# Four matmuls of a partition sum issued together, and a substitution issued in three runs, in the second mixer of a two-block transformer kernel

## The chip, the cores and the metric

The kernel runs on one core of a Trainium2 chip. The metric is device microseconds for one execution, which takes in two transformer blocks. TensorE (PE) does the matmuls, VectorE (DVE) and ScalarE (ACT) the elementwise work, GpSimd (POOL) hardly any; SyncE (SP) issues most DMAs. Each engine works through its own queue in order, and waits there for what its next instruction needs.

## The reference

Everything is float32, with 512 tokens and a model width of 1024. Two blocks follow each other; each is a feed-forward, a mixer and a feed-forward, with residuals and norms. The second block's mixer is the part that is changed. Its input projection has 28 slices of 128 columns (12 of a short convolution, 12 of q, k and v, 4 of z) and 8 columns for beta and the decay.

```python
def gated_delta_rule_chunked(q, k, v, g, beta):
    ...
    g = jnp.cumsum(g.reshape(bsz, n, c, nh).transpose(0, 3, 1, 2), axis=-1)
    decay = jnp.exp(jnp.where(causal, gdiff, -jnp.inf))
    lower = jnp.where(strict, jnp.einsum('bhncd,bhnsd->bhncs', k_beta, k) * decay, 0.0)
    rhs = jnp.concatenate([v_beta, k_beta * jnp.exp(g)[..., None]], axis=-1)
    sol = lax.linalg.triangular_solve(lower, rhs, left_side=True, lower=True, unit_diagonal=True)
    u, w = sol[..., :dv], sol[..., dv:]
    attn_intra = jnp.where(causal, jnp.einsum('bhncd,bhnsd->bhncs', q, k) * decay, 0.0)
    ...
    def step(state, inp):
        q_c, k_c, u_c, w_c, a_c, gl = inp
        v_new = u_c - jnp.einsum('bhck,bhkv->bhcv', w_c, state)
        o_c = jnp.einsum('bhck,bhkv->bhcv', q_c, state) + jnp.einsum('bhcs,bhsv->bhcv', a_c, v_new)
        state = state * gl[..., None, None] + jnp.einsum('bhck,bhcv->bhkv', k_c, v_new)
        return state, o_c
```

q, k and v go through a causal convolution of 4 taps and a silu; q and k are scaled to unit length per head (a sum of squares over the head's 128 channels, which lie on the partitions here); the head's output goes through an RMS norm (again such a sum) and a gate silu(z). The short convolution has 3 taps and a norm in 8 groups of 64 channels. There are 4 heads of 128 channels.

## The kernel before

A product of float32 matrices is made of three matmuls of split values (hi x wh, lo x wh, hi x wl), so that a projection of 1024 inputs by 128 outputs over 512 tokens is a pass of 24 matmuls (`gproj`, L819), each with 512 columns. A pass is read out by VectorE with the norm's scale (L1001, L1011, L1014, L1026). The weights of a pass arrive by DMA and are split by ScalarE (wh, L198) and VectorE (wl, L199).

In the second mixer (`mix2`) PE's order is written by hand. `main()` runs through the 28 passes and yields after each matmul; after each one `tick()` (L1042) steps at most one generator whose lag has run out. Such generators are the chain of a head (`chain`), of which up to three run at once, the end of a short convolution (`short_end`) and the decays. A generator issues work for all engines up to its next `yield`, and the number that it yields, out of the table `LAG`, is how many ticks (projection matmuls) go by before it is stepped again. The Tile scheduler puts the instructions of VectorE and ScalarE into an order of its own, fixed when the kernel is built.

A head's chain takes these steps, named by the lag behind them:

- entry: the decay (`decay`: spread of columns L267, gl L791, er L793, dec L796 and L799), transposes of k (L836), kd and ke (L838, L839), squares of k and q (c0);
- the key-query product L848, masked scores `at` (L850), q scaled by er (L851) (c1);
- the sum of squares of k, four matmuls of one column each (L714 in `tok_sums`), a reciprocal square root by Newton steps on VectorE (L240 to L253) (c2);
- the key-key product L864, u (L867) (c3), transposes of v L872, vi (L873) (c5);
- the preparation of the substitution of 16 x 16 blocks (L881 to L892), transposes of u L899 (c6);
- the substitution: products by block L905 and L906, evicted by ScalarE into bx (L907), then 15 turns of two small VectorE operations (L913, L915), then zu (L917) (c7);
- three merge levels (L925, L927, L932, L933, L937; zu renewed at L938) (c8, c9), the product with ke, L942, evicted as wt (L944) (c10);
- a scan over four groups of tokens: pv (L953, L955), vn (L956), po (L958, L967), pst (L962), st (L966) (r0, r1); the sum of squares of the output (o0), its spread and the gate (o1).

PSUM tiles with tag "g" share three banks (`bank`), which every step above asks for in turn; a step waits until the bank's last tile has been read. The silu and the exponential lie in different activation tables; an ACT_TABLE_LOAD stands ahead of an activation whose table is not the one loaded.

Of the kernel before, what the change touches and what calls it, by code (L numbers as in the profile page):

```python
# [30 lines left out]
LIVE = 3  # L31
NWARM = 9
SCRATCH = 1024
LAG = dict(d0=4, d1=30, d2=81, d3=7, d4=10, tok=1, c0=7, c1=3, c2=3, c3=2, c5=17, c6=26, c7=46, c8=11, c9=9, c10=11, r0=3, r1=4, o0=9, o1=27, s0=14, s1=22)
MIXORD = (4, 5, 6, 0, 1, 2, 3, 7)
WINDOWS = (2, 4, 8, 16)
MAGIC = float(0x5F3759DF)
# [87 lines left out]
class Kern:  # L125
# [4 lines left out]
    def nm(self, s):  # L130
        self.n += 1
        return f"{s}_{self.n}"
# [8 lines left out]
def tile_blocks(ctx: ExitStack, tc: tile.TileContext, ins, out, stop=None):  # L141
# [15 lines left out]
    ones1 = const.tile([P, 1], F32, name="ones1")  # L157
    gcomb = const.tile([P, 8], F32, name="gcomb")

    def vcol(name, i=0, n=1):  # L160
        o = VEC_COLS[name][0] + i
        return vec[:, o : o + n]
# [19 lines left out]
    def tmp():  # L182
        return tp.tile([P, T], F32, name=nm("t"), tag="t", bufs=5)

    def stmp():
        return tp.tile([P, T], F32, name=nm("s"), tag="s", bufs=3)
# [50 lines left out]
    def rsqrt_cols(src, n, scale, eps=EPS):  # L237

        v = rp.tile([P, n], F32, name=nm("rv"), tag="rv", bufs=4)
        nc.vector.tensor_scalar(v, src, scale, eps, ALU.mult, ALU.add)  # L240
        return newton(v, n)
# [411 lines left out]
    def mix2(prep, nxt):  # L653
# [3 lines left out]
        with ExitStack() as c:  # L657
            yp = K.pool(c, nm("yc"))
            yc, os_ = [None] * 4, [None] * GH
            with ExitStack() as c2:  # L660
# [12 lines left out]
                def gk(name, i=0):  # L673
                    o, n = CONST_COLS[name]
                    o += i * P - NKEEP
                    return gcst[:, o : o + min(n, P)]
# [3 lines left out]
                groups = gk("groups")  # L680
# [5 lines left out]
                def ct(n):  # L686
                    return cp.tile([P, n], F32, name=nm("c"), tag=f"c{n}", bufs={4: 12, 16: 10}[n])
# [5 lines left out]
                def bank(shape=S):  # L693
                    return psp.tile(shape, F32, name=nm("pg"), tag="g", bufs=3)
# [4 lines left out]
                def th(x):  # L699
                    return x.rearrange("p (t q) -> p t q", q=4)  # L700

                def hb(x):
                    return x.rearrange("p (o q) -> p o q", o=1).to_broadcast([P, NT, 4])
# [4 lines left out]
                def tok_sums(s, n, rhs):  # L708

                    ps = bank([P, NT, n])  # L710
                    for t in range(NT):
                        if t:
                            yield LAG["tok"]
                        nc.tensor.matmul(ps[:, t, :], s[:, t * P : (t + 1) * P], rhs, start=True, stop=True)  # L714
                    return ps

                def spread2(cols, groups=1):
                    ps = bank([P, T])
                    spread_into(ps, cols, groups)
                    return ps  # L720
# [18 lines left out]
                def decays():  # L739

                    yield LAG["d0"]
                    bas = tmp()
                    nc.vector.tensor_tensor(bas[:16], pba[:16], rb[:16], ALU.mult)
                    yield LAG["d1"]
                    pbt = bank([P, NT, 16])
# [26 lines left out]
                    nc.vector.scalar_tensor_tensor(th(g), th(z), -1.0, hb(ea), ALU.mult, ALU.mult)  # L772
                    yield LAG["d2"]

                    pg = bank([P, 16])
                    nc.tensor.matmul(pg, csum, g, start=True, stop=True)
                    nc.vector.tensor_copy(gc, pg)
                    yield LAG["d3"]
                    pg2 = bank([P, 16])
# [4 lines left out]
                    nc.scalar.activation(eg, gc, AF.Exp)  # L784
                    yield LAG["d4"]
                    decayed.append(True)
# [43 lines left out]
                def chain(hd, q, k, v):  # L830
# [9 lines left out]
                    sk = stmp()  # L840
# [11 lines left out]
                    yield LAG["c1"]  # L852

                    irk, es = ct(4), ct(4)
                    pn = yield from tok_sums(sk, 1, ones1)
                    rk = rsqrt_cols(pn.rearrange("p t o -> p (t o)"), NT, 1.0)
                    nc.vector.reciprocal(irk, rk)
                    nc.vector.tensor_tensor(es, rk, rk, ALU.mult)
# [49 lines left out]
                    zc = ep.tile([P, NT, SB], F32, name=nm("zc"), tag="zc", bufs=2)  # L908
                    nc.gpsimd.tensor_copy(zc, gk("d16").rearrange("p (o c) -> p o c", o=1).to_broadcast([P, NT, SB]))
                    for i in range(SB - 1):  # L910
                        sb = ep.tile([P, NT, SB], F32, name=nm("sb"), tag="sb", bufs=2)
                        n = SB - 1 - i
                        nc.vector.tensor_tensor(sb[:, :, :n], bx[:, :, i, i + 1 :],  # L913
                                                zc[:, :, i : i + 1].to_broadcast([P, NT, n]), ALU.mult)
                        nc.vector.tensor_tensor(zc[:, :, i + 1 :], zc[:, :, i + 1 :], sb[:, :, :n], ALU.add)  # L915
# [54 lines left out]
                    so = stmp()  # L970
                    nc.scalar.activation(so, po, AF.Square)
                    nc.vector.tensor_tensor(so, so, o, ALU.add)
                    nc.scalar.activation(o, po, AF.Copy)
                    yield LAG["o0"]
                    pn = yield from tok_sums(so, 1, ones1)
                    ro = rsqrt_cols(pn.rearrange("p t o -> p (t o)"), NT, 1.0 / P, EPS * EPS * P)
                    yield LAG["o1"]
                    pb = spread2(col1(ro))
# [4 lines left out]
                def short_end(i, yy):  # L983
                    sq = stmp()
                    nc.scalar.activation(sq, yy, AF.Square)
                    yield LAG["s0"]
                    pn = yield from tok_sums(sq, 2, groups)
                    cols = rsqrt_cols(pn.rearrange("p t o -> p (t o)"), 2 * NT, 1.0 / 64)
                    yield LAG["s1"]
                    pb = spread2(cols.rearrange("p (t o) -> p t o", o=2), 2)  # L990
                    nc.vector.scalar_tensor_tensor(yy, yy, vcol("conv_out_norm_2", i), pb, ALU.mult, ALU.mult)
                    yc[i] = yy
# [3 lines left out]
                def qkv_of(hd):  # L996
                    qkv = [None] * 3
                    for s in (1, 0, 2):
                        ps = yield from gproj(12 + 4 * s + hd)
                        x_ = tmp()  # L1000
                        nc.vector.tensor_tensor(x_, ps, rb, ALU.mult)  # L1001
                        y = conv(x_, "gdn_conv_w_2", 4 * s + hd, 4)
                        o = (gp if s == 0 else ep).tile([P, T], F32, name=nm("qkv"), tag="q" if s == 0 else "kv", bufs=4 if s == 0 else 3)
                        nc.scalar.activation(o, y, AF.Silu)
                        qkv[s] = o
                    waiting.append(Steps(chain(hd, *qkv)))

                def short_of(i):
                    pa = yield from gproj(4 + i)
                    ca = tmp()  # L1010
                    nc.vector.tensor_tensor(ca, pa, rb, ALU.mult)  # L1011
                    pb_ = yield from gproj(8 + i)
                    chh = tmp()
                    nc.vector.tensor_tensor(chh, pb_, rb, ALU.mult)  # L1014
                    nc.vector.tensor_tensor(chh, chh, ca, ALU.mult)
                    y = conv(chh, "conv_short_w_2", i, 3)
                    pc_ = yield from gproj(i)
                    nc.vector.tensor_tensor(y, y, rb, ALU.mult)
                    yy = yp.tile([P, T], F32, name=nm("yy"), tag="yy", bufs=4)
                    nc.vector.tensor_tensor(yy, pc_, y, ALU.mult)  # L1020
                    shorts.append(Steps(short_end(i, yy)))
# [66 lines left out]
    for what in ("x0", "w00", "x1", "x2", "x3", "w01", "x4", "x5", "x6", "w10", "w11", "x7"):  # L1088
# [4 lines left out]
        else:  # L1093
            i, j = int(what[1]), int(what[2])
# [115 lines left out]
```

## Time and profile before

| | |
|---|---|
| median of 3 runs | 2249.04 us (2247.82 to 2250.24) |
| profiled execution | 2249.06 us |
| its span | 2247.1 us |
| mean granted clock | 0.995 |
| PE busy | 2224.2 us, 99% |
| DVE busy | 1123.8 us, 50% |
| ACT busy | 814.5 us, 36% |

The span is the time between the first and the last instruction; 1.96 us of the execution lie outside it. The second mixer runs in it from 1569.9 us (first L819) to 1829.86 us (first L214 of the output projection). Busy is the time in which an engine worked on an instruction; a matmul's busy time overlaps that of the next, so that the distance of starts says what a matmul costs. The granted clock is that of TensorE, where 1.00 is full speed.

### The profile page before, as it was taken

The numbers are of one execution on the slowest core, as the hardware profiler recorded it, in microseconds if no ns is written. First come the engines' busy times: TensorE is split into PE (matmuls) and PEld (weight loads), VectorE is DVE, ScalarE is ACT, GpSimd is POOL, SyncE is SP. The second block draws the span as 40 slices with busy tenths as digits, with TensorE's granted clock in tenths as the row PEclk, the third lists the DMA queues.
The fourth block names the chain that finished last, engine by engine and source line by source line (L and its number), as shares of the span: only waits on it lengthen the run. The fifth ranks groups of instructions, "written<-read, shape, count | busy, mean of one in ns | idle before, by whom it ended". The sixth has DMA issues, their size and how long they took to land. (4 is left out here: it accounts for less than half of the span.)

```text
span 2247.1 us, 25204 instructions
## 1 busy us (share of the span) xinstructions
PE 2224.2 (99%) x10246; PEld 1847.2 (82%) x10246; DVE 1123.8 (50%) x1701; ACT 814.5 (36%) x1067; POOL 35.9 (2%) x54
## 2 busy tenths in 40 slices
PE   9999999999999999999999999999989999999998
PEld 7888888888888888888888888888778888888887
DVE  6444334565654455444434544433787665444332
ACT  6233223444432234332324332222565344233321
POOL 0000000000220000000000000000000000000000
PEclk9999999999999999999999999999999999999999
DMA  5333333322233232333332333333211123232332
GB/s 165 96 101 94 96 94 112 96 81 85 75 104 102 95 94 96 102 94 99 94 93 90 106 100 94 95 98 102 75 57 38 57 75 94 95 103 94 96 96 71
DMA packets 61476, 208.17 MB, mean 93 GB/s; under 512 B 6832, under 2 KB 9392, under 8 KB 61360
## 3 DMA queue, kind: packets, MB, share of 16 engines
q1 hardware_dynamic: 58832, 203.48, 29.2%
q10 hardware_dynamic: 2528, 3.08, 0.4%
q8 instruction: 80, 1.31, 0.2%
q14 instruction: 36, 0.29, 0.0%
HBM read 204.44 MB, written 2.10 MB: 92 GB/s over the span
## 5 line engine op out<-in xcount | busy, mean ns | idle before, releaser
L214 PE MATMUL ps<-hi,wh 128*128 128x512 f32 (+1 forms) x2774 | 1076.2, 388 | 1.4 <-ACT wh L198 1.3
L215 PE MATMUL ps<-lo,wh 128*128 128x512 f32 (+1 forms) x2774 | 1075.7, 388 | 0.3 <-DVE lo L202 0.3
L216 PE MATMUL ps<-hi,wl 128*128 128x512 f32 (+1 forms) x2774 | 1075.6, 388 | 0.0
L198 ACT ACTIVATE wh<-wr 128x1024 fp32r<-128x1024 f32 (+2 forms) x392 | 407.4, 1039 | 1135.3 <-PE ps L215 613.5
L199 DVE TENSOR_TENSOR wl<-wr,wh 128x1024 fp32r<-128x1024 f32 (+2 forms) x392 | 469.1, 1197 | 332.9 <-ACT wh L198 332.0
L214 PEld LDWEIGHTS ps<-hi,wh 128*128 128x128 f32 x2774 | 521.2, 188 | 109.5 <-ACT wh L198 2.4
L215 PEld LDWEIGHTS ps<-lo,wh 128*128 128x128 f32 x2774 | 521.1, 188 | 108.1 <-DVE lo L202 1.7
L216 PEld LDWEIGHTS ps<-hi,wl 128*128 128x128 f32 x2774 | 521.3, 188 | 107.4 <-DVE wl L199 1.2
L362 DVE TENSOR_TENSOR t<-ps,rb 128x512 f32<-128x512 f32 x88 | 60.8, 691 | 257.4 <-PE ps L216 257.4
L359 DVE TENSOR_TENSOR t<-ps,rb 128x512 f32<-128x512 f32 x88 | 60.8, 691 | 169.5 <-PE ps L216 169.4
L198 ACT ACTIVATE hi<-t 128x512 fp32r<-128x512 f32 x119 | 75.2, 632 | 114.6 <-DVE t L364 63.3
L819 PE MATMUL ps<-hi,wh 128*128 128x512 f32 x224 | 93.6, 418 | 0.3 <-DVE t L1001 0.3
L819 PE MATMUL ps<-hi,wl 128*128 128x512 f32 x224 | 93.0, 415 | 0.0
L819 PE MATMUL ps<-lo,wh 128*128 128x512 f32 x224 | 92.6, 413 | 0.0
L199 DVE TENSOR_TENSOR lo<-t,hi 128x512 fp32r<-128x512 f32 x119 | 83.5, 702 | 6.0 <-ACT hi L198 5.6
L364 DVE TENSOR_TENSOR t<-t,t 128x512 f32<-128x512 f32 x88 | 60.9, 692 | 8.3
L360 ACT ACTIVATE t<-t 128x512 f32<-128x512 f32 x88 | 54.1, 615 | 4.1 <-DVE t L359 4.1
L373 DVE SCALAR_TENSOR_TENSOR h<-ps,h 128x512 f32<-128x512 f32 x31 | 21.4, 692 | 60.4 <-PE ps L216 60.4
L819 PEld LDWEIGHTS ps<-hi,wh 128*128 128x128 f32 x224 | 43.2, 193 | 7.2 <-DVE t L1001 0.8
L819 PEld LDWEIGHTS ps<-hi,wl 128*128 128x128 f32 x224 | 43.2, 193 | 6.7 <-issue 0.2
L819 PEld LDWEIGHTS ps<-lo,wh 128*128 128x128 f32 x224 | 43.1, 192 | 6.6 <-issue 0.2
L808 DVE SCALAR_TENSOR_TENSOR t<-t,vec,t 128x511 f32<-128x511 f32 (+2 forms) x44 | 32.5, 744 | 0.2
(291 smaller groups left out, 1222.2 us busy)
## 6 DMA issues: line engine op xcount, KB each, us to landing
wr<-in_ffn_w_in SPq DMA_DIRECT2D x174, 512.0 KB, 3.5
wr<-in_ffn_w_out SPq DMA_DIRECT2D x64, 512.0 KB, 3.5
wr<-in_w_in SPq DMA_DIRECT2D x48, 512.0 KB, 3.5
wr<-in_w_mix_in SPq DMA_DIRECT2D x28, 512.0 KB, 3.5
wr<-in_ffn_w_out SPq DMA_DIRECT2D x32, 384.0 KB, 3.1
wr<-in_w_v SPq DMA_DIRECT2D x8, 512.0 KB, 3.6
wr<-in_w_ret_up SPq DMA_DIRECT2D x8, 512.0 KB, 3.5
wr<-in_w_pool_up SPq DMA_DIRECT2D x8, 512.0 KB, 3.5
```

Source lines behind the costliest of these rows:

```text
L198: nc.scalar.activation(hi, src, AF.Copy)
L199: nc.vector.tensor_tensor(lo, src, hi.bitcast(F32), ALU.subtract)
L214: nc.tensor.matmul(ps, lh, rh, start=start, stop=False)
L215: nc.tensor.matmul(ps, lh, rl, start=False, stop=False)
L216: nc.tensor.matmul(ps, ll, rh, start=False, stop=stop)
L359: nc.vector.tensor_tensor(g, pg, rb, ALU.mult)
L360: nc.scalar.activation(g, g, AF.Silu)
L362: nc.vector.tensor_tensor(u, pu, rb, ALU.mult)
L364: nc.vector.tensor_tensor(m, g, u, ALU.mult)
L373: nc.vector.scalar_tensor_tensor(h[d], ps, 0.5, h[d], ALU.mult, ALU.add)
L808: nc.vector.scalar_tensor_tensor(y[:, s:], x_[:, : T - s], vcol(names, (kw - 1 - s) * nt + i), y[:, s:], ALU.mult, ALU.add)
L819: nc.tensor.matmul(ps, a[:, k, :], b, start=(k == j == 0), stop=(k == KD - 1 and j == 2))
```

## The change

`tok_sums` issues its four matmuls in one step, with no yield between them, and is a plain function; its three callers (12 calls, 48 matmuls) take its result directly. The loop of 15 turns of the substitution yields before its turns 4 and 9 with the lag c7, which becomes 16 in place of 46; with the yield behind zu it now waits three times. Six other lags grow by 1 or 2, and `tok` goes.

```diff
--- before.py
+++ after.py
@@ -31,7 +31,7 @@
 LIVE = 3
 NWARM = 9
 SCRATCH = 1024
-LAG = dict(d0=4, d1=30, d2=81, d3=7, d4=10, tok=1, c0=7, c1=3, c2=3, c3=2, c5=17, c6=26, c7=46, c8=11, c9=9, c10=11, r0=3, r1=4, o0=9, o1=27, s0=14, s1=22)
+LAG = dict(d0=4, d1=30, d2=81, d3=7, d4=10, c0=9, c1=3, c2=3, c3=2, c5=19, c6=28, c7=16, c8=12, c9=9, c10=11, r0=3, r1=4, o0=10, o1=27, s0=14, s1=22)
 MIXORD = (4, 5, 6, 0, 1, 2, 3, 7)
 WINDOWS = (2, 4, 8, 16)
 MAGIC = float(0x5F3759DF)
@@ -709,8 +709,6 @@
 
                     ps = bank([P, NT, n])
                     for t in range(NT):
-                        if t:
-                            yield LAG["tok"]
                         nc.tensor.matmul(ps[:, t, :], s[:, t * P : (t + 1) * P], rhs, start=True, stop=True)
                     return ps
 
@@ -852,7 +850,7 @@
                     yield LAG["c1"]
 
                     irk, es = ct(4), ct(4)
-                    pn = yield from tok_sums(sk, 1, ones1)
+                    pn = tok_sums(sk, 1, ones1)
                     rk = rsqrt_cols(pn.rearrange("p t o -> p (t o)"), NT, 1.0)
                     nc.vector.reciprocal(irk, rk)
                     nc.vector.tensor_tensor(es, rk, rk, ALU.mult)
@@ -908,6 +906,8 @@
                     zc = ep.tile([P, NT, SB], F32, name=nm("zc"), tag="zc", bufs=2)
                     nc.gpsimd.tensor_copy(zc, gk("d16").rearrange("p (o c) -> p o c", o=1).to_broadcast([P, NT, SB]))
                     for i in range(SB - 1):
+                        if i in (4, 9):
+                            yield LAG["c7"]
                         sb = ep.tile([P, NT, SB], F32, name=nm("sb"), tag="sb", bufs=2)
                         n = SB - 1 - i
                         nc.vector.tensor_tensor(sb[:, :, :n], bx[:, :, i, i + 1 :],
@@ -972,7 +972,7 @@
                     nc.vector.tensor_tensor(so, so, o, ALU.add)
                     nc.scalar.activation(o, po, AF.Copy)
                     yield LAG["o0"]
-                    pn = yield from tok_sums(so, 1, ones1)
+                    pn = tok_sums(so, 1, ones1)
                     ro = rsqrt_cols(pn.rearrange("p t o -> p (t o)"), NT, 1.0 / P, EPS * EPS * P)
                     yield LAG["o1"]
                     pb = spread2(col1(ro))
@@ -984,7 +984,7 @@
                     sq = stmp()
                     nc.scalar.activation(sq, yy, AF.Square)
                     yield LAG["s0"]
-                    pn = yield from tok_sums(sq, 2, groups)
+                    pn = tok_sums(sq, 2, groups)
                     cols = rsqrt_cols(pn.rearrange("p t o -> p (t o)"), 2 * NT, 1.0 / 64)
                     yield LAG["s1"]
                     pb = spread2(cols.rearrange("p (t o) -> p t o", o=2), 2)
```

Lines behind the removed ones have numbers lower by 2: L819 becomes L817, L848 L846, L899 L897, L905 to L907 L903 to L905, L714 L712, L791 L789, L793 L791, L796 L794, L799 L797, L806 L804, L808 L806. The substitution's L913 to L917 and what follows keep theirs.

The change moves work on every engine. The first place is head 1's entry on ScalarE. Before, bx (L907) is evicted ahead of the entry's activations; `c`, `er`, `dec` are head 1's decay, `qkv_11431` its q and `qkv_11529` its v:

```order
L907 ACTIVATE bx_11464<-pg_11465 128x512
L907 ACTIVATE bx_11464<-pg_11469 128x512
L806 ACTIVATE t_11524<-t_11522,vec 128x512
L791 ACT_TABLE_LOAD
L791 ACTIVATE c_11544<-pg_11539 128x4
L1004 ACT_TABLE_LOAD
L1004 ACTIVATE qkv_11431<-t_11426 128x512
L1004 ACTIVATE qkv_11529<-t_11524 128x512
L793 ACT_TABLE_LOAD
L793 ACTIVATE er_11546<-pg_11539 128x512
L843 ACTIVATE o_11566<-qkv_11431 128x512
L799 ACTIVATE dec_11548<-dec_11548 128x512
```

After, where a table load and `c` of L789 stand directly ahead of the first of these rows (`qkv_11431` is q, `qkv_11471` is v):

```order
L1004 ACT_TABLE_LOAD
L1004 ACTIVATE qkv_11431<-t_11426 128x512
L804 ACTIVATE t_11466<-t_11464,vec 128x512
L791 ACT_TABLE_LOAD
L791 ACTIVATE er_11488<-pg_11481 128x512
L841 ACTIVATE o_11508<-qkv_11431 128x512
L1004 ACT_TABLE_LOAD
L1004 ACTIVATE qkv_11471<-t_11466 128x512
L797 ACT_TABLE_LOAD
L797 ACTIVATE dec_11490<-dec_11490 128x512
L905 ACTIVATE bx_11512<-pg_11513 128x512
L905 ACTIVATE bx_11512<-pg_11517 128x512
```

The two evictions of bx have moved from ahead of the entry's activations to behind them, and v's silu is no longer beside q's.

The second place is the end of head 0's substitution on VectorE. `zu_11520` and `zu_11660` are head 0's zu, `ps` is the result of a projection pass, `u_11623` is head 1's. Before:

```order
L915 TENSOR_TENSOR zc_11473<-zc_11473,sb_11517 128x4
L873 TENSOR_TENSOR vi_11561<-pg_11630,c_11586 128x512
L917 TENSOR_TENSOR zu_11520<-zc_11473,gcst_10892 128x512
L859 TENSOR_TENSOR c_11587<-c_11587,c_10915 128x4
L867 SCALAR_TENSOR_TENSOR u_11623<-pg_11618,c_11587,dec_11548 128x128 x4
L883 COPY c_2051_11663<-u_11623 32x128 x2
L886 TENSOR_SCALAR c_2052_11668<-c_2051_11663,gcst_10892 128x64
L887 SCALAR_TENSOR_TENSOR c_2052_11668<-c_2051_11663,gcst_10892,c_2052_11668 128x64
L199 TENSOR_TENSOR lo_11672<-c_2052_11668,hi_11671 128x64
L892 TENSOR_TENSOR xx_11675<-hi_11671,gcst_10892 128x1024
L892 TENSOR_TENSOR xx_11677<-lo_11672,gcst_10892 128x1024
L1001 TENSOR_TENSOR t_11714<-ps_11650,rb_10905 128x512
```

After:

```order
L1001 TENSOR_TENSOR t_11698<-ps_11630,rb_10905 128x512
L913 TENSOR_TENSOR sb_11651<-bx_11512,zc_11521 128x4x3
L199 TENSOR_TENSOR wl_11883<-wr_11880,wh_11882 128x1024
L915 TENSOR_TENSOR zc_11521<-zc_11521,sb_11651 128x4x3
L806 SCALAR_TENSOR_TENSOR t_11700<-t_11698,vec,t_11700 128x511
L913 TENSOR_TENSOR sb_11654<-bx_11512,zc_11521 128x4x2
L806 SCALAR_TENSOR_TENSOR t_11700<-t_11698,vec,t_11700 128x510
L915 TENSOR_TENSOR zc_11521<-zc_11521,sb_11654 128x4x2
L806 SCALAR_TENSOR_TENSOR t_11700<-t_11698,vec,t_11700 128x509
L913 TENSOR_TENSOR sb_11657<-bx_11512,zc_11521 128x4
L915 TENSOR_TENSOR zc_11521<-zc_11521,sb_11657 128x4
L917 TENSOR_TENSOR zu_11660<-zc_11521,gcst_10892 128x512
```

Before, zu stands ahead of u and of the scaling of a pass (L1001); after, it stands behind the scaling, the weight split and the convolution of a pass, with the last three turns of the substitution among them.

The third place is PE at head 0's first merge level (L925), which reads that zu. Before:

```order
L819 MATMUL ps_11650<-hi_10773,wh_11646 128x512
L819 MATMUL ps_11650<-lo_10774,wh_11646 128x512
L819 MATMUL ps_11650<-hi_10773,wl_11647 128x512
L819 MATMUL ps_11650<-hi_10866,wh_11646 128x512
L925 MATMUL pg_11696<-zu_11520,lt_11415 128x128 x4
L927 MATMUL pg_11697<-cst,zu_11520 128x128 x4
L819 MATMUL ps_11650<-lo_10867,wh_11646 128x512
L819 MATMUL ps_11650<-hi_10866,wl_11647 128x512
```

After:

```order
L817 MATMUL ps_11630<-hi_10866,wh_11626 128x512
L817 MATMUL ps_11630<-lo_10867,wh_11626 128x512
L817 MATMUL ps_11630<-hi_10866,wl_11627 128x512
L817 MATMUL ps_11713<-hi_10217,wh_11709 128x512
L817 MATMUL ps_11713<-lo_10218,wh_11709 128x512
L817 MATMUL ps_11713<-hi_10217,wl_11710 128x512
L925 MATMUL pg_11717<-zu_11660,lt_11416 128x128 x4
L927 MATMUL pg_11718<-cst,zu_11660 128x128 x4
```

Before, the merge stands within the pass `ps_11650`, two matmuls ahead of its end; after, it stands three matmuls into the pass that follows `ps_11630`, the pass whose scaling is ahead of zu on VectorE.

## Rows read from the trace of the kernel before

**Rows 1.** The page's first part: busy time, share of the span and instructions of each engine.

```profile
PE 2224.2 (99%) x10246; PEld 1847.2 (82%) x10246; DVE 1123.8 (50%) x1701; ACT 814.5 (36%) x1067; POOL 35.9 (2%) x54
```

**Rows 2.** The second mixer in windows. Columns: the stretch in us, its length, busy us (and instructions) of PE, of PE's weight loads, of VectorE, of ScalarE and of GpSimd, granted TensorE clock, share of the DMA engines, GB/s.

```profile
1630.00:1660.00 30.00, 26.06 (x124) 21.46 (x123) 25.63 (x81) 15.98 (x26) 0.24 (x1) 0.89 0.15 54
1660.00:1690.00 30.00, 27.85 (x172) 24.15 (x171) 23.93 (x68) 18.62 (x31) 0.24 (x1) 1.00 0.17 54
...
1720.00:1750.00 30.00, 26.37 (x164) 23.43 (x163) 22.65 (x75) 15.02 (x28) 0.00 (x0) 0.94 0.11 36
```

**Rows 3.** The table of waits of the second mixer, 1569 to 1850 us, PE's rows alone. Columns: the engine and the line that waited, what it waited for, us in total, times, longest.

```profile
PE pv L955 <- DVE st L966: 3.6, 1, 3.6
...
PE pg L848 <- ACT qkv L1004: 2.2, 1, 2.2
...
PE pg L899 <- DVE u L867: 1.7, 1, 1.7
...
PE pg L927 <- ACT wt L944: 1.1, 1, 1.1
...
PE pg L942 <- DVE dec L796: 0.9, 1, 0.9
```

**Rows 4.** PE's timeline from the transposes of head 1's u to head 0's first merge level. Columns: start in us, us, engine, line, operation, out<-in, tile sizes, count [idle before <-releaser].

```profile
1652.34 1.10 PE L899 MATMUL pg<-cst,u 128*128 128x128 f32 x4 [1.70 <-DVE u L867]
...
1654.09 0.63 PE L819 MATMUL ps<-hi,wl 128*128 128x512 f32 x1
1654.52 0.63 PE L819 MATMUL ps<-hi,wh 128*128 128x512 f32 x1
...
1656.61 0.39 PE L819 MATMUL ps<-hi,wl 128*128 128x512 f32 x1
...
1657.08 0.49 PE L925 MATMUL pg<-zu,lt 128*128 128x128 f32 x3
```

**Rows 5.** PE's timeline, the same columns, at head 1's key-query product.

```profile
1639.23 1.87 PE L848 MATMUL pg<-qkv,qkv 128*128 128x128 f32 x8 [2.25 <-ACT qkv L1004]
...
1644.34 0.40 PE L819 MATMUL ps<-hi,wh 128*128 128x512 f32 x1
```

**Rows 6.** PE's timeline at the key-query product of head 2.

```profile
1679.53 1.06 PE L848 MATMUL pg<-qkv,qkv 128*128 128x128 f32 x8
1680.35 0.47 PE L819 MATMUL ps<-hi,wh 128*128 128x512 f32 x1
```

**Rows 7.** PE's timeline at a sum over partitions of head 0, and at the sums of the last norm (L423), where several stand in a run.

```profile
1616.68 0.48 PE L819 MATMUL ps<-hi,wh 128*128 128x512 f32 x1
...
1617.14 0.48 PE L819 MATMUL ps<-lo,wh 128*128 128x512 f32 x1
...
2229.82 0.36 PE L423 MATMUL pc<-ones,s 128*128 128x1 f32 x2
2230.04 0.36 PE L423 MATMUL pc<-ones,acc 128*128 128x1 f32 x2
```

**Rows 8.** PE's timeline at the scan of head 1 beside head 3's entry.

```profile
1730.27 0.49 PE L955 MATMUL pv<-st,wt 128*128 128x128 f32 x2 [3.63 <-DVE st L966]
...
1735.05 0.47 PE L819 MATMUL ps<-lo,wh 128*128 128x512 f32 x1
```

**Rows 9.** ScalarE's timeline at head 1's entry.

```profile
1634.08 1.06 ACT L907 ACTIVATE bx<-pg 128x512 f32<-128x512 f32 x2
1635.03 0.72 ACT L806 ACTIVATE t<-t,vec 128x512 f32<-128x512 f32 x1
1635.77 1.28 ACT L791 ACT_TABLE_LOAD   x1
1637.06 0.17 ACT L791 ACTIVATE c<-pg 128x4 f32<-128x4 f32 x1
...
1638.55 1.26 ACT L1004 ACTIVATE qkv<-t 128x512 f32<-128x512 f32 x2
...
1641.11 0.60 ACT L793 ACTIVATE er<-pg 128x512 f32<-128x512 f32 x1
```

**Rows 10.** PE's timeline behind the pass that ends at 1633.15, at head 1's entry.

```profile
1633.15 0.39 PE L905 MATMUL pg<-xx,bdr 128*128 128x512 f32 x1
...
1634.08 0.39 PE L819 MATMUL ps<-hi,wh 128*128 128x512 f32 x1
1634.31 0.60 PE L267 MATMUL pg<-cst,c 128*128 128x128 f32 x4
...
1635.12 0.47 PE L819 MATMUL ps<-lo,wh 128*128 128x512 f32 x1
```

**Rows 11.** VectorE's timeline where head 0's substitution ends.

```profile
1651.05 0.68 DVE L917 TENSOR_TENSOR zu<-zc,gcst 128x512 f32<-128x512 f32 x1
```

**Rows 12.** VectorE's timeline behind a projection pass, where head 1's substitution has ended.

```profile
1675.42 0.69 DVE L917 TENSOR_TENSOR zu<-zc,gcst 128x512 f32<-128x512 f32 x1
1676.04 0.68 DVE L1001 TENSOR_TENSOR t<-ps,rb 128x512 f32<-128x512 f32 x1
1676.75 1.22 DVE L199 TENSOR_TENSOR wl<-wr,wh 128x1024 fp32r<-128x1024 f32 x1
1677.89 0.74 DVE L808 SCALAR_TENSOR_TENSOR t<-t,vec,t 128x511 f32<-128x511 f32 x1
1678.55 0.68 DVE L938 TENSOR_TENSOR zu<-zu,pg 128x512 f32<-128x512 f32 x1
```

## The prediction

> **What bounds the kernel now.** I read the page's first part, then the windows of the second mixer, then the table of waits, then the engines' timelines around the waits of PE. Over the whole span PE is busy 99% [rows 1], so only time in which PE stands still, or runs slowly, can be won or lost. The mixer's PE order is fixed by hand; VectorE and ScalarE follow in a queue order that is fixed too. In the windows the reader is to see three stretches of 30 us in which PE falls short of full: 26.06, 27.85 and 26.37 us, two of them with a granted clock under 1.00 [rows 2]. The table of waits names what lies there: five waits of PE, 3.6, 2.2, 1.7, 1.1 and 0.9 us, together 9.6 us [rows 3]. After three of them PE also runs on at a lower clock: behind the 1.70 us wait the projection matmuls start 0.43 us apart (1654.09 to 1654.52), and 0.23 apart again from 1656.61 [rows 4]. I work that loss out as the time from the end of a wait to where full pitch is back, less the same work at full pitch. Behind the 2.25 wait: 1639.23 to 1644.34 is 5.1 us [rows 5], holding eight key-query matmuls (0.82 at full clock [rows 6]), seven projections at 0.227 and four small sums at 0.23 [rows 7], 3.3 us: 1.8 lost. Behind the 1.70 wait: 1652.34 to 1656.61 is 4.3 us for 2.2 us of work: 2.1 lost. Behind the 3.63 wait: 1730.27 to 1735.05 is 4.8 us for 3.1 us: 1.7 lost [rows 8]. After the 0.9 and 1.1 us waits the window's clock stays 1.00 [rows 2]. So the mixer loses 9.6 + 5.6 = 15.2 us in waits of PE and what follows them. That is the most the change can bring.
>
> **The change, part by part.**
>
> *The sums in one run.* Twelve calls, 48 matmuls, the same number before and after. Between projections one costs 0.46 less 0.227, so 0.23 us (the starts at 1616.68 and 1617.14); in a run, 0.22 (2229.82 to 2230.04) [rows 7]. Forty-eight times 0.01 is half a microsecond at most; I take -0.3. What the run does change is timing: it asks for its PSUM bank, and all of its input, in one place.
>
> *Where things now stand.* The lags add up to nearly the same ticks, but head 1's chain entry now comes with the substitution of head 0 still to be done (its two-matmul products move behind the entry's transposes), and the first merge level of head 0 moves from two projection matmuls ahead of the end of a pass to three matmuls into the next one. The moved steps issue no DMA, and of GpSimd only the copy that starts zc. Each removed wait is looked at for what comes next.
>
> *Head 1's entry.* In the old order ScalarE evicts the substitution's input (bx) first, at 1634.08 [rows 9], and then has three table loads up to er. In the new order five table loads and seven other activations stand in front of bx: c, silu q, the scaling of v's convolution, er, the square of q, silu v, exp of the decay. The sum's bank is the one that the first bx eviction frees. ScalarE is free for this at 1634.1; a load to the next activation takes 1.29 us (1635.77 to 1637.06), c 0.2, q and v 0.63 each (1638.55, two in 1.26), the convolution's scaling 0.7, er 0.5, the square and the decay 0.6 each, the first bx 0.5 [rows 9]: 5 x 1.29 + 4.4 = 10.8, so 1644.9. PE asks for that bank after 13 projection matmuls (2.95), the entry's spread and transposes (0.81, 1634.31 to 1635.12), four products (0.93, 1633.15 to 1634.08) and the key-query product (0.82, as before), from 1633.15 [rows 10]: 1638.7. PE must therefore lose 6.3 us up to there, whether in one wait or in three (on the bank of ke, on er and the decay ahead of the key-query product at about 1640.0, and on bx). Some low clock follows the last wait; I take 7.0 in all, 5.0 if part of the activations overlap, 8.5 with a full clock loss as in [rows 4]. The waits that go in return are the 2.25 us one and, since VectorE is now relieved of the interleaved substitution, the 1.70 us one on u.
>
> A rule of the Trainium skill, page "ScalarE: Activation LUTs", section "What ACT_TABLE_LOAD costs", puts a switch of sets at about 2.66 us, a load and a drain of 1.38. The rows here show the next activation 1.29 us after the load's start, with no drain to be seen [rows 9], so the measurement decides; by the page's figure five switches would put bx 6.9 us later, and the same section's consequence, that switches between sets are to be few, speaks against this change, since the new order has two more.
>
> *The first merge level of head 0.* Before, zu is written at 1651.05 and read at 1657.08, so nothing waits [rows 4, 11]. In the new VectorE order zu stands behind the scaling of a projection pass that ends only three matmuls ahead of the merge. From the start of the pass's last matmul: 0.45 to its end, scaling 0.62, the split of weights 1.14 (and about 0.2 for its wait on ScalarE), three convolution taps of 0.66, three pairs of small operations about 0.3, zu 0.66 [rows 12]: 5.3. PE comes to it after 4 x 0.227 = 0.9. The wait is 4.4 at least; I take 5.0, since VectorE also starts the substitution late (bx only at about 1645.4). A wait of this size brings a clock loss like those of [rows 4, 5, 8], 1.9 more. Behind that matmul all of PE is queued, so the 6.9 are all paid. Bounds 5.0 and 7.9. The old 0.9 and 1.1 us waits at head 2's entry fall away with the shift of their neighbours, and the order puts others there: the sum's bank behind the decay's last read, about 0.5, and the product with ke behind the masked scores, about 0.7. I take 1.2, from 0.5 to 2.9.
>
> *The product with ke of head 1* (L942) then stands behind the last zu update, which stands behind the scaling, the weight split and the three taps of a pass ending ten matmuls and one merge product earlier: 0.45 + 0.62 + 1.14 + 0.2 + 2.0 + 0.6 = 5.0 against 2.27 + 0.82 = 3.1 (the product as at 1679.53 [rows 6]): 1.9, with some small operations between 2.0, and a clock loss as at [rows 8] of up to 1.7. I take 3.5; 1.9 to 3.7.
>
> *The scan of head 1 beside head 3's entry.* Before, it holds the 3.63 us wait for st [rows 8]. The scan's step now comes a little earlier than the entry's decay, and st waits behind two transposed copies, three taps and the decay for about 0.5, then vn behind a table load, 1.29 at the most on its own [rows 9]. I take 1.5, from 0.5 to 3.6 (the old wait unchanged in size and without its clock loss).
>
> *Sum.* Removed 15.2. Added 7.0 + 6.9 + 1.2 + 3.5 + 1.5 - 0.3 = 19.8. Net +4.6 on the profiled execution's 2249.06 us, which stands 0.02 above the median: 2253.7. With the low ends (5.0 + 5.0 + 0.5 + 1.9 + 0.5 - 0.5 = 12.4) it is 2246.3, with the high ends (8.5 + 7.9 + 2.9 + 3.7 + 3.6 = 26.6) 2260.5.
>
> **The rivals.**
>
> *First, not slower: the entry is cheap.* Its place is head 1's entry, its deciding point whether the run of sums finds a bank free without bx. Then only the key-query product waits for er and the decay, 1640.0 against 1637.2 = 2.8, and no second wait prolongs the low clock: 2253.7 - 4.2 = 2249.5, or 2246 with the scan's step at its low end and no loss of clock at L942. For it: three banks rotate and which one is asked for is a matter of one position. Against: the order puts bx behind all five loads, and all three banks are held by the entry.
>
> *Second, faster: all five waits go and nothing takes their place*, 2249.1 - 15.2 = 2233.9, or with only the first merge level late 2240.8. For it: every wait of before stands where VectorE carried 30 interleaved substitution operations among the entry's work, and that mixing is gone. Against: zu's place behind a fresh pass is in the order itself.
>
> *Third, the change does nothing to the time*: the sums cost the same [rows 7], and the new waits are of the size of the old. 2249, give or take 3.
>
> *Fourth, slower: the loads take longer than the rows show.* With five loads at twice the 1.29 us the entry costs 6.5 more: 2260.2. Against: the loads in these rows read 1.28 and hold the engine for 1.29 [rows 9]. The figure of the Trainium skill (page "ScalarE: Activation LUTs") weighed above is this case.
>
> **How the numbers follow.** Two runs of this kernel differ by up to 0.1%, and I call 0.2% (4.5 us) the smallest difference that a measurement can tell: faster is under 2244.5, slower over 2253.5. Forecast 0.60, of which 0.37 lie above 2253.5 and 0.23 within; first rival 0.17 (0.13 within, 0.04 faster); second 0.08 (faster); third 0.11 (0.09 within, 0.02 slower); fourth 0.04 (slower). Faster 0.12, same 0.45, slower 0.43. The range runs from 2245, which takes in the first and third rivals and the low ends, to 2260.5; left out are the second rival and the upper tail. The forecast's own range is 2249.5 to 2260.
>
> **What would show it.** In the table of waits after: PE waiting for zu from L917 at the first merge level for 4 us or more; PE waiting at head 1's entry, 6 us in sum, with bx or er as releaser and five table loads in a row ahead of bx; a wait of about 2 us at L942; the waits on silu q and on u gone. The granted clock of the 30 us around head 1's entry and the merge should be at or under 0.89. I am wrong if PE comes through the entry with under 3 us of waits, or if the merge level starts without one.

## The result and the profile after

The changed kernel takes 2259.66 us (median of 6 runs, 2258.47 to 2260.83) against 2248.40 for the kernel before (6 runs): a ratio of 1.0051, 95% interval 1.0040 to 1.0061. It is slower by 11 us, clear of the 0.2% that a measurement can tell. The forecast was 2253.7 us in a range of 2245 to 2260.5, with 0.43 for slower and 0.45 for no difference. The profiled execution took 2258.88 us, 9.8 more than that of before.

PE's busy time hardly changes, 2225.4 us on the page of after, 1.2 more than in [rows 1], so what was added is again PE standing still or running slowly.

Two windows of the second mixer after the change, around head 1's entry and the first merge level, columns as in [rows 2]:

```profile
1630.00:1660.00 30.00, 22.21 (x108) 17.67 (x106) 25.28 (x78) 18.58 (x25) 0.00 (x0) 0.94 0.17 53
1660.00:1690.00 30.00, 25.36 (x140) 21.91 (x141) 20.38 (x59) 13.39 (x24) 0.47 (x2) 0.89 0.16 53
```

In the first window PE is busy 22.21 us where it was 26.06 [rows 2], and in the next 25.36 where it was 27.85. The mixer, from its first projection matmul to the first of the output projection, lasts 1570.04 to 1839.41, 269.4 us; before it was 259.7 (1570.15 to 1829.86; the 1569.9 given ahead is the start of that matmul's weight load). So 9.7 of the 9.8 us lie in it. PE's rows of the table of waits:

```profile
PE pg L925 <- DVE zu L917: 5.6, 1, 5.6
...
PE pst L962 <- ACT vn L956: 2.7, 4, 1.1
...
PE pg L846 <- DVE dec L794: 2.6, 1, 2.6
...
PE pg L942 <- DVE sb L913: 2.2, 1, 2.2
...
PE pg L903 <- DVE ke L837: 1.5, 1, 1.5
PE pg L712 <- ACT bx L905: 1.5, 1, 1.5
...
PE pg L712 <- DVE dec L794: 1.2, 1, 1.2
...
PE pv L955 <- DVE st L966: 0.2, 1, 0.2
```

None of the five rows of [rows 3] is left: the waits on silu q, on u, on wt and (L942) on the decay are gone, and st is down from 3.6 to 0.2 us. In their place stand a 5.6 us wait for zu at the first merge level, three waits at head 1's entry (1.5 for ke ahead of the second half of head 0's block products, 2.6 for the decay ahead of the key-query product, 1.5 for bx ahead of the sums), 2.2 at L942, 1.2 for the sums of head 2 and 2.7 in four places for vn. The releaser named in the row of L942 is one of the small operations; by the order, what PE needs there is zu's last update (L938), which stands next to it on VectorE.

Head 1's entry on ScalarE, with [rows 9] as its counterpart:

```profile
1633.72 1.28 ACT L789 ACT_TABLE_LOAD   x1
...
1635.21 1.28 ACT L1004 ACT_TABLE_LOAD   x1
...
1637.76 1.28 ACT L791 ACT_TABLE_LOAD   x1
...
1640.19 1.28 ACT L1004 ACT_TABLE_LOAD   x1
...
1642.13 1.28 ACT L797 ACT_TABLE_LOAD   x1
1643.43 0.63 ACT L797 ACTIVATE dec<-dec 128x512 f32<-128x512 f32 x1
1643.96 1.07 ACT L905 ACTIVATE bx<-pg 128x512 f32<-128x512 f32 x2
```

The reader is to see five loads, from 1633.72 on, with the activations that they serve between them and no idle time named in any row, and bx only at 1643.96. The last load gives way to the decay's exponential after 1.30 us. PE's timeline beside it:

```profile
1636.35 0.47 PE L903 MATMUL pg<-xx,bdr 128*128 128x512 f32 x1 [1.49 <-DVE ke L837]
...
1641.29 1.13 PE L846 MATMUL pg<-qkv,qkv 128*128 128x128 f32 x8 [2.63 <-DVE dec L794]
...
1644.60 1.05 PE L712 MATMUL pg<-ones,s 128*128 128x1 f32 x8 [1.48 <-ACT bx L905]
```

The sums get their bank at 1644.60, 0.6 us behind the start of the bx evictions. The forecast had 1644.9.

VectorE and PE at the first merge level:

```profile
1656.87 1.22 DVE L890 TENSOR_TENSOR xx<-lo,gcst 128x1024 fp32r<-128x1024 f32 x1
...
1658.10 0.68 DVE L1001 TENSOR_TENSOR t<-ps,rb 128x512 f32<-128x512 f32 x1
...
1658.77 1.22 DVE L199 TENSOR_TENSOR wl<-wr,wh 128x1024 fp32r<-128x1024 f32 x1
...
1659.99 0.74 DVE L806 SCALAR_TENSOR_TENSOR t<-t,vec,t 128x511 f32<-128x511 f32 x1
...
1662.62 0.69 DVE L917 TENSOR_TENSOR zu<-zc,gcst 128x512 f32<-128x512 f32 x1
```

```profile
1657.42 0.39 PE L817 MATMUL ps<-hi,wl 128*128 128x512 f32 x1
1663.45 2.05 PE L925 MATMUL pg<-zu,lt 128*128 128x128 f32 x8 [5.64 <-DVE zu L917]
...
1667.43 0.41 PE L817 MATMUL ps<-hi,wh 128*128 128x512 f32 x1
```

zu ends at 1663.3 and PE starts at 1663.45. Scaling, weight split and three taps of the pass (the first at 1659.99) stand ahead of it, as the order had shown. VectorE came to the scaling at 1658.10, 1.0 us behind the pass's end (its last matmul starts at 1656.74, three ahead of the one at 1657.42, and takes 0.39), since it was still at the block preparation (L890).

What the waits leave behind is read from the granted clock in short windows (columns as above):

```profile
1637.00:1647.00 10.00, 5.89 (x37) 4.68 (x36) 6.29 (x21) 7.94 (x11) 0.00 (x0) 1.00 0.17 53
1647.00:1650.00 3.00, 3.00 (x13) 2.51 (x12) 2.67 (x20) 0.00 (x0) 0.00 (x0) 0.50 0.01 3
1663.50:1667.00 3.50, 3.50 (x14) 3.31 (x15) 0.00 (x0) 1.59 (x6) 0.17 (x1) 0.50 0.00 0
1691.50:1694.50 3.00, 3.00 (x15) 2.90 (x14) 2.50 (x14) 2.45 (x5) 0.00 (x0) 0.50 0.00 0
1726.40:1730.00 3.60, 3.57 (x20) 3.12 (x21) 3.05 (x17) 1.15 (x2) 0.00 (x0) 1.00 0.00 0
1742.50:1745.50 3.00, 3.00 (x15) 2.81 (x14) 1.52 (x9) 0.00 (x0) 0.00 (x0) 0.51 0.28 113
```

Four stretches run at 0.50, the 1.2 GHz level. By the same count as in the prediction (time less work at full pitch) they lose 1.8 us (1646.28 to 1650.34), 2.1 (1663.45 to 1667.43), 1.7 (1691.35 to 1694.74) and 1.7 (1742.51 to 1745.88): 7.3, where before it was 5.6.

Put together: PE's waits are 18.9 us by the whole table against 10.7 before, 8.2 more; the clock costs 1.7 more; the sums give back 1.3 (four in a run take 0.81 us, 1739.76 to 1740.57, against 4 x 0.23). That is 8.6 of the 9.7. Most of the other 1.1 lies in how a row counts: it starts at the modelled end of the matmul ahead, 0.39 us behind its start, while at full pitch the next one starts 0.23 behind it, so that each wait costs some 0.16 us more than its row. The tables hold 15 waits after and 10 before, which makes 0.8 by this estimate; the rest was not followed.

```profile
1739.76 0.95 PE L712 MATMUL pg<-ones,s 128*128 128x1 f32 x8
1740.57 0.48 PE L817 MATMUL ps<-lo,wh 128*128 128x512 f32 x1
```

### The profile page after: what moved, and what is told of

Same layout as the page of the kernel before. It is cut to its first block, busy times and chain, and to the rows that moved or that the text cites. A ratio compares the mean times of both kernels' runs of the same rounds, so it can differ in the third digit from the quotient of the medians.

```text
span 2256.9 us, 25206 instructions
## 1 busy us (share of the span) xinstructions
PE 2225.4 (99%) x10246; PEld 1848.1 (82%) x10246; DVE 1124.6 (50%) x1701; ACT 817.4 (36%) x1069; POOL 36.0 (2%) x54
## 5 line engine op out<-in xcount | busy, mean ns | idle before, releaser
L817 PE MATMUL ps<-lo,wh 128*128 128x512 f32 x224 | 92.4, 412 | 0.0
L817 PE MATMUL ps<-hi,wh 128*128 128x512 f32 x224 | 91.7, 409 | 0.3 <-DVE t L1001 0.3
L817 PE MATMUL ps<-hi,wl 128*128 128x512 f32 x224 | 91.6, 409 | 0.0
L817 PEld LDWEIGHTS ps<-hi,wh 128*128 128x128 f32 x224 | 43.0, 192 | 7.7 <-DVE t L1001 0.8
L817 PEld LDWEIGHTS ps<-hi,wl 128*128 128x128 f32 x224 | 43.2, 193 | 7.1 <-issue 0.2
L817 PEld LDWEIGHTS ps<-lo,wh 128*128 128x128 f32 x224 | 42.9, 192 | 7.1 <-issue 0.5
L806 DVE SCALAR_TENSOR_TENSOR t<-t,vec,t 128x511 f32<-128x511 f32 (+2 forms) x44 | 32.5, 744 | 1.2 <-ACT t L804 1.0
```

The source lines that it names most:

```text
L806: nc.vector.scalar_tensor_tensor(y[:, s:], x_[:, : T - s], vcol(names, (kw - 1 - s) * nt + i), y[:, s:], ALU.mult, ALU.add)
L817: nc.tensor.matmul(ps, a[:, k, :], b, start=(k == j == 0), stop=(k == KD - 1 and j == 2))
```

## The experiments

Theory after the result: the longer lags c0, c5 and c6 move head 0's block products past head 1's entry; that one crossing puts bx behind five loads, and zu behind a fresh pass, that is a pass whose last matmul PE has issued just ahead of the merge. Rivals: the substitution in three runs does it by itself; the sums in one run do it by themselves, since they ask for a bank and all of their input at once.

**One lag back.**

```diff
-c6=28
+c6=26
```

> The changed kernel with one number put back: the lag c6 is 26 instead of 28, so that head 0's block products come back in front of head 1's entry. Theory (order at head 1's entry): the lags c0, c5 and c6, two ticks longer each, carry those products past the entry; bx is then evicted behind five table loads, which makes both the entry's waits and the late merge level. Then here bx stands ahead of the loads again, the entry's waits fall to under 2 us, the merge's to under 2.5 us, and the time comes to 2242 to 2249 us. Rival 1 (the substitution in three runs puts zu behind a fresh pass): the merge's 5.6 us wait stays, 2255 us or more. Rival 2 (the sums in one run ask for a bank too early): the wait of the sums stays, 2256 to 2260.

Measured: 2248.16 us, ratio to before 0.9996 (0.9987 to 1.0004). Both edits of the program are in it, and the whole loss is gone. ScalarE's timeline shows why, and PE's rows of the waits the two largest that are left (two of 1.2 us for the sums' banks and one of 1.1 for st follow them):

```profile
1633.72 0.60 ACT L905 ACTIVATE bx<-pg 128x512 f32<-128x512 f32 x1
...
1635.05 0.58 ACT L905 ACTIVATE bx<-pg 128x512 f32<-128x512 f32 x1
...
1636.17 1.28 ACT L789 ACT_TABLE_LOAD   x1
...
1637.54 0.59 ACT L791 ACTIVATE er<-pg 128x512 f32<-128x512 f32 x1
```

```profile
PE pst L962 <- ACT vn L956: 3.1, 4, 1.1
...
PE pg L925 <- DVE zu L917: 2.4, 1, 2.4
```

bx is out at 1635.6, ahead of every load of the entry, and up to the decay's exponential there are three loads instead of five, since silu q comes ahead of c and er follows c on the same table. The merge waits 2.4 us instead of 5.6. On VectorE zu now stands ahead of the pass's scaling:

```profile
1655.31 0.69 DVE L917 TENSOR_TENSOR zu<-zc,gcst 128x512 f32<-128x512 f32 x1
1655.91 0.69 DVE L1001 TENSOR_TENSOR t<-ps,rb 128x512 f32<-128x512 f32 x1
```

**One tick between.**

```diff
-c6=28
+c6=27
```

> The changed kernel with c6 = 27, one tick more than the run that was back at 2248 us with 26, one less than the change's 28. Theory (the order of head 0's block products and head 1's entry decides): with 27 the entry still goes first, so bx stays behind the entry's loads: 2253 to 2259 us, waits at the entry of 3 us or more and at the merge of 4 us or more; nearly all of the step lies between 26 and 27. Rival (time grows with the lags a little at a time, about 5.5 us a tick): 2254 at 27 with both waits halved, and no jump in the order of bx against the loads.

Measured: 2258.71 us, 1.0047 (1.0035 to 1.0060). From 26 to 27 the time rises by 10.5 us, from 27 to 28 by one. On ScalarE, bx again stands behind the five loads:

```profile
1643.97 1.06 ACT L905 ACTIVATE bx<-pg 128x512 f32<-128x512 f32 x2
```

The entry waits 4.5 us in all and the merge 6.1. It is a crossing, not a slope.

**The substitution in one run.**

```diff
-                        if i in (4, 9):
-                            yield LAG["c7"]
...
-c7=16
+c7=48
```

> The changed kernel with the substitution in one run again (no yields inside it, c7 = 48, so the merge keeps its tick); the sums stay in one run and the other lags as changed. Theory (order at head 1's entry): bx still stands behind five loads, so the entry's waits of about 5.5 us stay and the merge still waits for zu, 4 us or more, since the turns start only behind bx: 2254 to 2260 us. Rival 1 (the three runs): the merge's wait goes, 2247 to 2252. Rival 2 (the sums in one run): about as the changed kernel, 2257 to 2260, with the wait of the sums for bx.

Measured: 2258.06 us, 1.0045 (1.0032 to 1.0057). The entry's waits are the same to the tenth (1.5, 2.6, 1.5). The merge's falls to 2.9, where 4 or more was expected: zu still stands behind the scaling and the weight split of the fresh pass, but ahead of its three taps, behind which the three runs had put it (line numbers from the loop on are lower by 2 here):

```profile
1659.88 0.68 DVE L915 TENSOR_TENSOR zu<-zc,gcst 128x512 f32<-128x512 f32 x1
1660.48 2.31 DVE L806 SCALAR_TENSOR_TENSOR t<-t,vec,t 128x511 f32<-128x511 f32 x3
```

The whole table of PE's waits falls only from 18.9 to 16.6 us, and the profiled executions take the same (2258.97 and 2258.88); what makes up the difference was not followed. So the three runs lengthen the merge's wait, but they did not bring the loss.

**Both edits at the old ticks** (the difference to the change; c7z is the lag behind zu):

```diff
-c0=9, c2=3, c5=19, c6=28, c7=16, c8=12, o0=10, o1=27, s1=22
+c0=7, c2=6, c5=17, c6=26, c7=16, c7z=14, c8=11, o0=9, o1=30, s1=25
```

> Both edits of the program (sums in one run, substitution in three) with the steps at the ticks of the kernel before: c0, c5, c6, c8, o0 as before, the lags behind a sum three longer, the three waits of the substitution 16, 16 and 14, together 46. Theory (order at head 1's entry): nothing crosses the entry, so the time is that of the kernel before, 2245 to 2251, with the 2.2 us wait of the key-query product for silu q and the 3.6 us one for st still there. Rivals 1 and 2: 2254 or more, since both edits are in it.

Measured: 2250.80 us, 1.0005 (0.9996 to 1.0014). The old waits are back (3.6 for st, 2.2 for silu q). The merge waits 2.4 us for zu, which I had not expected here, and little goes away elsewhere (u 1.3 instead of 1.7): the whole table of PE's waits is 12.6 us against 10.7 before, and the profiled execution 1.8 us longer.

**Each edit alone.** The substitution in three runs, on the kernel before:

```diff
-c7=46
+c7=16, c7z=14
...
+                        if i in (4, 9):
+                            yield LAG["c7"]
```

> The kernel before with the substitution alone in three runs (16, 16 and 14 ticks, together the 46 of before); sums and lags as before. Theory (order at head 1's entry): 2243 to 2249; the wait for u behind head 1's entry gets shorter (from 1.7 to about 1 us), since fewer of the turns are mixed into the entry, the others stay. Rival 1 (the three runs cost): 2253 or more, with a wait for zu at the first merge level. Rival 2 expects the time of before, 2248.

Measured: 2248.02 us, 0.9996 (0.9987 to 1.0005); u waits 0.7 instead of 1.7. And the sums in one run, on the kernel before:

```diff
-c2=3, o1=27, s1=22
+c2=6, o1=30, s1=25
...
-                        if t:
-                            yield LAG["tok"]
```

> The kernel before with the sums alone in one run; the lags behind a sum are three longer, so that every later step keeps its tick. Theory (only the order at the entry matters): 2247 to 2252, the five waits of before with about their sizes; the run itself gives back about 1 us at most (0.20 us a matmul in a run against 0.23 between projections, 48 of them). Rival (the run asks for its bank and its input too early): a new wait of the sums of over 1 us, 2253 or more.

Measured: 2250.29 us, 1.0011 (1.0002 to 1.0019), with no wait of the sums; u's wait comes in three pieces, 2.6 us in all, and one of 1.5 stands at the output projection. At the old lags, neither edit alone moves the median by 2 us.

**bx on VectorE.** All lags as changed.

```diff
-                        nc.scalar.activation(bx[:, 2 * b : 2 * b + 2], pb, AF.Copy)
+                        nc.vector.tensor_copy(bx[:, 2 * b : 2 * b + 2], pb)
```

> The changed kernel with bx copied out of PSUM by VectorE instead of ScalarE (two copies of 512 columns for each head, some 0.6 us each), all lags as changed. It takes bx out of the queue behind the five table loads, and leaves zu behind the scaling of the fresh pass. Theory in two parts (bx behind the loads costs the entry; zu behind a fresh pass costs the merge): the entry's waits fall from 5.6 us to about 1 to 2, the merge's wait stays at 3.5 us or more, 2250 to 2255 us. Rival (late bx alone makes both waits): the merge's wait falls under 2 us too, 2245 to 2249. Rival (the loads are beside the point, PE's own order costs the time): 2257 to 2260, entry's waits as before.

Measured: 2251.80 us, 1.0014 (1.0005 to 1.0023), 7.9 us less than the change.

```profile
PE pg L925 <- DVE zu L917: 5.6, 1, 5.6
...
PE pg L846 <- DVE dec L794: 2.6, 1, 2.6
...
PE pg L903 <- DVE ke L837: 1.5, 1, 1.5
```

```profile
1638.32 1.05 PE L846 MATMUL pg<-qkv,qkv 128*128 128x128 f32 x8
...
1639.91 0.95 PE L712 MATMUL pg<-ones,s 128*128 128x1 f32 x8
```

```profile
1635.94 0.68 DVE L905 COPY bx<-pg 128x512 f32<-128x512 f32 x1
...
1658.31 0.69 DVE L917 TENSOR_TENSOR zu<-zc,gcst 128x512 f32<-128x512 f32 x1
```

VectorE starts on bx at 1635.94, where ScalarE came to it at 1643.96. At head 1's entry the key-query product (1638.32) and the sums (1639.91) now start without a wait, although ScalarE has the same five loads; the 1.5 us for ke stay, and 0.35 us are new at the key-key product. That is 1.8 us in place of 5.6, the 1 to 2 that the theory expected. The key-query product starts before the decay's first read (1640.10 in this run), so it no longer takes the bank that those reads free; by the order, the bank that it takes is one of bx's. Late bx thus held both the key-query product and the sums. The row of 2.6 us at L846 is not this entry's: it stands at 1684.88, at head 2's entry, where the change had 1.2 us ahead of the sums.

The merge's wait stays at 5.6 although bx is early: zu still stands behind the pass's scaling (1654.20), so that place is enough for it, and late bx is not needed. The wait at L942 also went; why was not tried. The profiled execution, at the high end of its runs, is 5.3 us below that of the change, and the whole table of PE's waits 4.6 lower (14.3). bx is moved for all four heads here, and the reverse, late bx with zu ahead of the scaling, was not tried.

**A version with more room.** c6 = 26, sums in one run, substitution in one run, and the readers of the remaining waits set later:

```diff
-c6=28, c7=16, c9=9, r0=3, o1=27, s0=14
+c6=26, c7=48, c9=12, r0=4, o1=30, s0=16
```

> A version meant to beat both: sums in one run, substitution in one run, c6 = 26 (bx ahead of the entry's loads), and the other lags spread so that the waits that are left have more room: c9 12 instead of 9 (the merge's updates), r0 4 instead of 3 (vn of the scan), o1 30 instead of 27, s0 16 instead of 14, c7 48. The run with c6 = 26 alone still had waits of 3.1 us for vn, 2.4 for zu, 1.1 for st and 2.4 for the sums' banks, 9 us, and some 4 us of low clock behind them. Theory (waits are set by what each engine's queue holds ahead, and go when the reader comes later): about two thirds of these 13 us go, 2236 to 2243 us, no wait of PE over 2.2 us. Rival (the waits only move on, since the chain has as much to do): 2246 to 2250.

Measured: 2237.55 us (2237.10 to 2237.90), 0.9951 (0.9938 to 0.9965). It beats both kernels. PE's waits in the mixer:

```profile
PE pg L897 <- DVE u L865: 0.9, 1, 0.9
PE pg L935 <- DVE dec L794: 0.9, 1, 0.9
PE pg L712 <- DVE sb L911: 0.9, 1, 0.9
```

No wait reaches 1 us, and the granted clock is 1.00 in all windows from 1630 to 1750 us. How much each of the changed lags gave was not separated. With the substitution in three runs:

```diff
-c7=48, c10=11
+c7=14, c7z=20, c10=7
...
+                        if i in (4, 9):
+                            yield LAG["c7"]
```

> As the retimed version, but with the substitution in three runs (14, 14 and 20 ticks, together 48) and c10 = 7. Theory (the three runs neither cost nor win by themselves once bx is in time): within 4 us of the retimed version with one run, 2237 to 2245. Rival (three runs put zu late behind fresh passes): a wait for zu of 2 us or more and 2246 or more.

Measured: 2240.35 us, 0.9966 (0.9954 to 0.9979); the merge waits 2.2 us for zu, so the rival's wait is there, but not its time. It is 2.8 us above the version with one run, and no run of either lies in the other's range: here the three runs cost a little. And, from the version with one run, with c6 = 28:

```diff
-c6=26
+c6=28
```

> The retimed version with one substitution, with c6 = 28 again in place of 26, and nothing else. Theory (the crossing of head 0's block products and head 1's entry decides, whatever the other lags are): bx behind the five loads, waits of over 5 us at the entry and over 3 us at the merge come back, 10 us or more above the retimed version, 2248 to 2258. Rival (the added room takes up the crossing): less than 4 us above it.

Measured: 2254.32 us, 1.0025 (1.0016 to 1.0035), 16.8 above. The five loads are ahead of bx again; the entry waits 1.0, 3.1 and 0.6, the merge 2.9, all a little under what I wrote. A wait of 4.4 us for the columns of a norm (L267, at 1834.58, by the end of the mixer) is new, as are 1.6 and 0.8 at other merge levels (1684.14 and 1693.32), so not all of the 16.8 lies at the crossing.

## Why the prediction was right, and where its sizes were off

The measured time lies in the range, but 0.8 us from its upper end: the forecast had +4.6 and the kernel lost 11.3. Term by term:

*Removed, 15.2 us.* Right: all five waits went, the 3.6 us one but for 0.2.

*Head 1's entry, 7.0.* Waits 5.6 and 1.8 of clock, 7.4. The chain of five loads gave the sums' start within 0.3 us. The cause named there was the cause: with bx on VectorE, and the five loads as before, the waits of the key-query product and of the sums are gone, and the 1.5 for ke is left, with 0.35 new. Of the signs, the entry's waits are 5.6 where 6 was named, and the granted clock at or under 0.89 held for the merge's window (0.89), not for the entry's (0.94).

*First merge level, 6.9.* 5.6 and 2.1, 7.7. The place behind the fresh pass was right, as the run with bx on VectorE showed; VectorE came to that pass 1.0 us late, for which I had 0.6, held by the block preparation and not by bx.

*Head 2's entry, 1.2.* The wait is 1.2, but the match is luck: I had 0.5 for the sums' bank and 0.7 for the product with ke, and all of it stands at the sums. And 1.7 of low clock follows it, which only the high end held.

*Product with ke, 3.5.* The wait is 2.2 (forecast 2.0), but no clock loss follows: 2.2.

*The scan, 1.5 (0.5 to 3.6).* This is the step that failed most: 2.9 us of waits for vn and st and 1.7 of clock, 4.6. I counted one table load ahead of vn in head 1's scan. There are two waits there: in the first (0.70) vn stands behind a convolution's scaling and er, in the second (1.13) behind two loads, a silu and the decay's exponential, all of them late, since ScalarE had waited 2.27 us for VectorE's taps ahead of the first load. Two more waits for vn (0.60 and 0.25) lie in other heads' scans, for which I had no term.

```profile
1738.00 1.28 ACT L1004 ACT_TABLE_LOAD   x1 [2.27 <-DVE t L806]
...
1741.78 0.35 ACT L956 ACTIVATE vn<-pv,c 128x128 f32<-128x128 f32 x1
```

*The sums, -0.3.* They gave 1.3, estimated from the one run of 0.81 us, twelve times.

The terms come to 23.5 where the forecast had 19.8; with the 1.1 that no row carries, that is 4.8 of the 5.2 between +4.6 and the profiled +9.8. The median's +11.3 is 1.4 above this: the profiled execution is 0.8 below the median of its six runs, and that of before 0.7 above its own.

*The rivals.* The cheap entry fell: the sums did wait for bx. (The 2246 given for it adds up to 2246.9.) No change in the time, 2249 give or take 3, fell too. All waits going with nothing in their place fell in the change, yet it is what the retimed version reaches in large part, 10.6 us below before against the 15.2 on offer. Loads longer than the rows fell: here too the next activation starts 1.29 us after a load, so by these rows the drain that the Trainium skill adds ("ScalarE: Activation LUTs", "What ACT_TABLE_LOAD costs") does not appear. The rule of the Trainium skill to batch activations by table set, which the prediction puts into the section on the cost, stands on the same page ("ScalarE: Activation LUTs") in "Table sets: the hidden batching unit". The trace agrees so far as five switches with the work between them took 10.2 us (1633.72 to 1643.96), 6.4 of it loads; what it costs depends on what stands behind them, as with the same five loads the run with bx on VectorE is 7.9 us faster.

## What to carry to other kernels

In a pipeline whose engines each follow a fixed queue, look for pairs of steps whose order a lag can flip, and at what then stands ahead of the reader on every engine: here one tick in one lag moved an eviction from ahead of the table loads to behind five of them, and zu from ahead of a fresh pass's scaling to behind it, and cost 10 us, while each edit alone, at the old lags, moved the time by under 2. Ask of each producer whether it stands behind work that cannot start until just before its reader; then no slack ahead of it helps.

## What was not expected of the hardware

The clock after a wait does not follow from the length of that wait alone. After the 2.19 us wait at 1726.43 the granted clock stays at 1.00; after waits of 1.19 us (1689.91) and 1.13 us (1742.18) it is 0.50 and 0.51 shortly behind. At the entry PE was busy only 5.89 of 10 us (1637 to 1647) at a clock of 1.00, and the 0.50 came behind it, when PE was at work without a wait.
